# A second set of residual staging tiles for the down projection, kept in a quarter of the up projection's result

## The chip, the cores and the metric

The kernel runs on all 8 NeuronCores of one Trainium2 chip: two dies, cores 0 to 3 and cores 4 to 7. The cores share no data. The time of a run is that of its slowest core, in microseconds (us) on the device.

Runs come in two states. In the slow one, a die (sometimes both) runs at a lower granted TensorE clock (the share of full clock that the profile's clock record shows) and the run is longer. In the first job, the slowest run after the change took 5593.35 us, with die 0 at 0.812 or 0.813 and die 1 at 0.991 or 0.992. The fast runs are those in which no die is disturbed: the two after the change in that job took 4757.07 and 4761.27 us, with 0.990 to 0.994 on all cores.

## The reference, cut to what matters

The program is two layers of a mixed diffusion backbone. Only the end of each layer matters here, the MLP with its residual:

```python
    # channel mixer: squared-ReLU MLP
    h2 = _rms(x) * (1 + sc2) + sh2
    x = x + g2 * (jnp.square(jax.nn.relu(h2 @ w_ff1)) @ w_ff2)
```

`D_MODEL` is 2048, `D_FF` is 8192, and each core has 1280 tokens. The kernel does `D_FF` in four quarters `q`. For each it computes 2048 hidden channels (up projection), then adds their contribution to `x` (down projection).

## The kernel before

The kernel is a graph of operations that a list scheduler in Python puts into a fixed order for each of five engines, using guessed durations. Each list is then the program of its engine, in that order, with the semaphore waits in it. For a transfer the scheduler guesses this:

```python
                st = max(now + o.dur + 1.2, dma_free[0])
                en = st + o.dma / self.bw          # bw = 320e3 bytes per us
                dma_free[0] = en
                o.t1 = en + 0.9
```

For the 160 KB transfers that matter here that is about 2.7 us: 0.08 issue, 1.2 + 0.9 fixed, 0.51 for 163,840 bytes. On core 0 of the profile before, the medians from issue to landing were 6.0 us for these loads and 6.3 us for the spills.

Both projections use a Strassen-like scheme, seven block products in place of eight. A unit makes 2 x 128 output channels for all 1280 tokens: 7 products x 2 token halves x 8 chunks = 112 matmuls of 128x128 by 128x320. A down projection is 8 units.

```python
                prods = (("P", w8(ra, 0), ra, "B11", True), ("Q", w8(ra, 1), ra, "B21", True), ("P", k8(s2), s2, 1, False), ("R", k8(s1), s1, 0, True),
                         ("P", k8(s3), s3, 2, False), ("P", w8(rb, 1), rb, 3, False), ("R", k8(s4), s4, "B22", False))
```

The operand (`act`, 16 rows of 1280 columns) is read as the quarters B11, B21 and B22 and as four sums. The quarter B12, rows 0 to 7, columns 640 to 1280, is read only when the sums are made. After that its space is free. The kernel uses B12 of the up projection's operand `hT` as eight staging tiles for the residual `x`, which lives in DRAM (`xs`). Each unit loads eight pieces of `x`, adds the product on VectorE (DVE), and spills them back:

```python
            XSt = [hT[:, i, 640:1280].bitcast(F32) for i in range(8)]
            # ... (res: x = product * gate + x on DVE)
            def pre_f2(ba, bb):                       # before a unit: its eight loads
                for s_ in range(2):
                    for k, (blk, c) in enumerate(((ba, s_ * SUBS), (ba, 640 + s_ * SUBS), (bb, s_ * SUBS), (bb, 640 + s_ * SUBS))):
                        load(XSt[s_ * 4 + k], xs[blk][:, c:c + SUBS], 128 * SUBS * 4, r=xkeys(blk, c, SUBS), prio=S.p + 50, tag="xld")

            def epi_f2(dst):
                def f(blk, c, b, ps, s_, k):          # when a block of the product is done
                    x = XSt[s_ * 4 + k]
                    res(x, b, ps, *gcol(blk), c)
                    spill(blk, c, SUBS, x, dst)
                return f
```

Loads and spills are all issued by SyncE, in one program order. Weights are issued by GpSimd. Seven of the eight down projections (56 units) use these tiles. The last one of layer 0 works on tiles that stay in SBUF.

Of the kernel before, what the change touches and what calls it, by code (L numbers as in the profile page):

```python
# [8 lines left out]
F32 = mybir.dt.float32  # L9
# [473 lines left out]
T = 1280  # L483
# [46 lines left out]
def build():  # L530
# [36 lines left out]
    xs = nc.dram_tensor("xs", [16, 128, T], F32, kind="Internal").ap()  # L567
# [5 lines left out]
    with es:  # L573
        arena = es.enter_context(nc.sbuf_tensor("arena", [128, int(TOTKB * 512)], F16))
        psum = es.enter_context(nc.psum_tensor("psum", [128, 4096], F32))
        S = Graph(nc, es)

        def A(kb, shape, dt=F16):
            n = 1
            for s in shape:  # L580
                n *= s
            o = int(round(kb * 512))
            ne = n * DSZ[dt] // 2
            assert o + ne <= int(TOTKB * 512), (kb, shape)
            v = arena[:, o:o + ne]
            if dt != F16:
                v = v.bitcast(dt)
            if len(shape) == 1:
                return v
            if len(shape) == 2:  # L590
                return v.rearrange("p (a b) -> p a b", a=shape[0])
            return v.rearrange("p (a b c) -> p a b c", a=shape[0], b=shape[1])
# [62 lines left out]
        hT = A(0, [16, T])  # L655
# [25 lines left out]
        def load(dst, src, nb, q="sp", r=(), w=None, prio=None, tag="ld"):  # L681
            return S.dma(q, dst, src, nb, r=r, w=[dst] if w is None else w, prio=(S.p if prio is None else prio) - 60.0, tag=tag)
# [1111 lines left out]
        SUBS = 320  # L1794

        def xkeys(fc, t0, n):
            return ["xs%d_%d" % (fc, j) for j in range(t0 // SUBS, (t0 + n - 1) // SUBS + 1)]
# [5 lines left out]
        def spill(fc, t0, n, src, dst=None):  # L1803
            d = xs if dst is None else dst
            S.dma("sp", d[fc][:, t0:t0 + n], src, 128 * n * 4, r=[src], w=xkeys(fc, t0, n) if dst is None else [], tag="xst")
# [5 lines left out]
        def tsums(act, Ts, i):  # L1811
            b11, b12 = act[i][:, 0:640], act[i][:, 640:1280]
            b21, b22 = act[i + 8][:, 0:640], act[i + 8][:, 640:1280]
            t1, t2, t3, t4 = (t[:, i, :] for t in Ts)
            for o, x, y in ((t1, b12, b11), (t3, b22, b12), (t2, b22, t1), (t4, b21, t2)):
                tt("dve", o, x, y, ALU.subtract, 640, [x, y], [o], x=2)
# [90 lines left out]
        def layer(l):  # L1907
# [61 lines left out]
            def epi_f1(blk, c, b, ps, s_, k):  # L1969
# [9 lines left out]
                i = blk % 8  # L1979
                if done1.get(i, 0) == 4 and done1.get(i + 8, 0) == 4:  # L1980
                    tsums(M, ATs, i)
            XSt = [hT[:, i, 640:1280].bitcast(F32) for i in range(8)]

            def res(x, b, ps, g0, g1, c):

                cuts = [(0, SUBS, 0)] if c < 960 else [(0, 64, 0), (64, SUBS, 1)]
                for (u, v, s) in cuts:
                    i = b[:, u:v] if b is not None else (lambda u=u, v=v: ps.ap()[:, u:v])
                    g = (g0, g1)[s]
                    stt_(x[:, u:v], i, g, x[:, u:v], ALU.mult, ALU.add, v - u, [b if b is not None else ps, x[:, u:v]], [x[:, u:v]], ps=b is None, boost=BOOST)  # L1990

            def gcol(blk):
                return [modT[l][:, s, 80 + blk:80 + blk + 1] for s in range(2)]

            def pre_f2(ba, bb):
                for s_ in range(2):
                    for k, (blk, c) in enumerate(((ba, s_ * SUBS), (ba, 640 + s_ * SUBS), (bb, s_ * SUBS), (bb, 640 + s_ * SUBS))):
                        load(XSt[s_ * 4 + k], xs[blk][:, c:c + SUBS], 128 * SUBS * 4, r=xkeys(blk, c, SUBS), prio=S.p + 50, tag="xld")

            def epi_f2(dst):  # L2000
                def f(blk, c, b, ps, s_, k):
                    x = XSt[s_ * 4 + k]
                    res(x, b, ps, *gcol(blk), c)
                    spill(blk, c, SUBS, x, dst)
                return f
# [16 lines left out]
            for q in range(4):  # L2022
                done1 = {}
                if not last:
                    if q == 0:
                        mod_push(1, (0, 1, 2))
                    mod_spread(12, 9.0)
                pair1 = lambda i: (i, i + 8, w1[l, q * 16 + i], w1[l, q * 16 + i + 8])
                pair2 = lambda i: (i, i + 8, w2[l, q, i], w2[l, q, i + 8])
                if q == 0:  # L2030
                    head = [0, 8, 1, 9, 2, 10]
                    b1 = [(b, w1[l, b]) for b in head]
                    dense(b1[:5], H, ev_f1, group=5, tag="ff1")
                    dense(b1[5:], H, ev_f1, tag="ff1")
                    for i in range(3):
                        tsums(M, ATs, i)
                    sunits([pair1(i) for i in range(3, 8)], H, HTs, epi_f1, tag="sf1")
                else:
                    sunits([pair1(i) for i in range(8)], H, HTs, epi_f1, tag="sf1")
                if q < 3 or last:  # L2040
                    sunits([pair2(i) for i in range(8)], M, ATs, epi_f2(None if q < 3 else y_o), pre=pre_f2, tag="sf2")
                else:
                    reload_x(range(8), xs, True)
                    sunits([(i, i + 4, w2[l, q, i], w2[l, q, i + 4]) for i in range(4)], M, ATs, epi_x, tag="sf2")
                    reload_x((10, 11, 12, 13, 8, 9, 14, 15), xs, True)
                    e2 = ev_res(l, 80, after_x)
                    dense([(b, w2[l, q, b]) for b in (10, 11, 12)], M, e2, tag="ff2")
                    dense([(b, w2[l, q, b]) for b in (13, 8, 9, 14, 15)], M, e2, group=5, tag="ff2")
# [3 lines left out]
        for l in range(NL):  # L2052
            layer(l)
# [226 lines left out]
```

## Time and profile before

| | before |
|---|---|
| fast runs of the first job | 4810.74, 4820.74, 4815.32 us |
| core 0, an undisturbed core of the profiled run | span 4831.3 us, TensorE busy 4604.6 us |
| its idle time before the product line L1882 | 45.5 us |
| waits of DVE for loads of `xs` | 159.1 us |
| waits of SyncE for spills to `xs` to land | 379.9 us |

The profiled run of before was in the slow state: die 1 was throttled (median clock of its cores 0.930, against 0.983 on die 0). So the readings come from core 0, on die 0. Its page, part 5 (out<-in, shape, count, then busy us and mean ns, then the idle time before the group and what ended most of it), says of the MLP's matmuls and of the group with DVE's residual additions (it holds some other work of the same line too):

```profile
L1882 PE MATMUL psum<-arena 128*128 128x320 f16 x13216 | 1832.5, 302 | 45.5 <-ACT arena L770 38.9
...
L759 DVE SCALAR_TENSOR_TENSOR arena<-arena 128x320 f32<-128x320 f32 (+11 forms) x677 | 359.7, 556 | 297.5 <-DMA arena<-xs 136.7
```

The view of waits of the same core has, for DVE and for SyncE (us in total, times, longest):

```profile
DVE arena L759 <- DMA arena<-xs: 159.1, 133, 6.0
SPq L438 <- DMA xs<-arena: 379.9, 217, 14.0
```

TensorE waited 45.5 us here, 38.9 of them for a ScalarE copy that frees a PSUM bank (PSUM is what the matmuls write, `psum<-arena`). That copy is not the cause. In the first down projection (1601 to 1734 us) DVE's biggest wait is for loads of `xs`, 30.0 us, and the ScalarE copies in turn wait longest for DVE's additions, 64.7 us. The cause shows when the chain of waits is followed back. Part 4 for the same core:

```profile
## 4 chain that ended last, share of the span: by engine, by line
PE 77%; DMA 16%; DVE 2%; issue 2%; SPq 2%; ACT 1%; POOL 1%; DVEq 0%; ACTq 0%; POOLq 0%
```

And a piece of that chain within the first down projection (start us, us, what):

```profile
1614.23 8.34 DMA xs<-arena
1622.56 0.02 issue
...
1622.63 0.32 SPq L222
...
1623.04 6.85 DMA xs<-arena
...
1630.36 8.29 DMA xs<-arena
...
1639.13 6.07 DMA xs<-arena
...
1645.26 6.43 DMA arena<-xs
...
1651.78 0.06 DVE arena L759
```

For 37 us nothing but transfers decides the time. A spill lands, SyncE (`SPq L222`) issues the load that stood waiting for it, then the spill that stood behind that load, and so on. In the end DVE waits for a load.

### The profile page before, as it was taken

To read this page: it belongs to the slowest core of one execution; us is meant where nothing else is said; L and a number is where in the kernel's file an instruction comes from. 1 tells how busy PE (TensorE), PEld (TensorE's weight loads), DVE (VectorE), ACT (ScalarE), POOL (GpSimd) and SP (SyncE) were. 2 spreads that over 40 slices of the span, in tenths; PEclk is the share of its full clock that TensorE was granted. 3 is DMA by queue.
4 is the path that set the end of the run, shared out by engine and by line. 5 is a ranking of instruction groups with operands and counts; after the bars stand their busy time and mean duration, and the time that the engine had idled before them with its cause. 6 is when DMAs were issued, how large, how long until landed. Compare 5 with 4: busy or idle time off the path is not lost.

```text
span 5042.2 us, 91205 instructions; the slowest of 8 cores (4811.6 to 5042.2 us)
## 1 busy us (share of the span) xinstructions
PE 4866.5 (97%) x31452; PEld 2977.5 (59%) x31452; DVE 2633.1 (52%) x5454; ACT 1791.0 (36%) x3781; POOL 506.9 (10%) x916
## 2 busy tenths in 40 slices
PE   3989999999999999999999999999999999999999
PEld 2544455556655666666654545555565566666666
DVE  4266645565454545454563565556553555454545
ACT  2235333332235242333443353333321532424151
POOL 1131210001001010000011301000010000000000
PEclk9989999999889989898899999999998899989899
DMA  9873763447857877878777645334666457474837
GB/s 206 133 137 84 151 109 69 84 85 144 175 121 120 189 144 169 164 148 177 149 174 129 120 107 103 64 71 85 133 114 175 95 117 177 101 192 81 213 65 197
DMA packets 339444, 664.37 MB, mean 132 GB/s; under 512 B 51888, under 2 KB 210352, under 8 KB 338992
## 3 DMA queue, kind: packets, MB, share of 16 engines
q0 software_dynamic: 106848, 368.10, 44.9%
q1 hardware_dynamic: 232144, 290.45, 18.3%
q8 instruction: 259, 4.24, 0.4%
q14 instruction: 193, 1.58, 0.1%
HBM read 894.07 MB, written 132.38 MB: 204 GB/s over the span
## 4 chain that ended last, share of the span: by engine, by line
PE 90%; DMA 5%; DVE 2%; issue 1%; SPq 1%; ACT 1%; POOL 0%; DVEq 0%; ACTq 0%; POOLq 0%
PE psum L1882 37%; PE psum L693 23%; PE psum L1698 17%; PE psum L1663 5%; PE psum L1219 1%; PE psum L827 1%; PE psum L1094 1%; DMA arena<-wm 1%; DMA xs<-arena 1%; PE psum L1076 1%; DMA arena<-lc 1%; DMA arena<-wg 1%; DVE arena L755 1%; SPq L222 1%; PE psum L1096 1%
## 5 line engine op out<-in xcount | busy, mean ns | idle before, releaser
L1882 PE MATMUL psum<-arena 128*128 128x320 f16 x13216 | 1980.2, 318 | 3.7 <-ACT arena L770 3.7
L1882 PEld LDWEIGHTS psum<-arena 128*128 128x128 f16 x13216 | 1357.1, 103 | 621.7 <-issue 15.7
L755 DVE TENSOR_TENSOR arena<-arena 128x1024 f16<-128x1024 f16 (+10 forms) x2162 | 1073.8, 519 | 692.2 <-PE psum L1882 354.3
L693 PE MATMUL psum<-arena 128*128 128x512 f16 (+2 forms) x6272 | 1284.9, 368 | 12.9 <-DVE arena L759 7.3
L744 ACT ACTIVATE arena<-arena 128x320 f16<-128x320 f32 (+12 forms) x1679 | 832.6, 515 | 906.4 <-DVE arena L755 517.0
L755 DVE TENSOR_TENSOR arena<-psum,arena 128x320 f32<-128x320 f32 (+3 forms) x1406 | 684.0, 490 | 825.0 <-PE psum L1882 263.3
L693 PEld LDWEIGHTS psum<-arena 128*128 128x128 f16 x6272 | 635.4, 103 | 615.4 <-issue 297.3
L1698 PE MATMUL psum<-arena 128*128 128x320 f16 x6272 | 973.7, 306 | 15.4 <-ACT arena L744 10.1
L770 ACT COPY arena<-psum 128x320 f32<-128x320 f32 (+5 forms) x987 | 422.9, 435 | 1378.0 <-PE psum L1882 725.0
L1698 PEld LDWEIGHTS psum<-arena 128*128 128x128 f16 x6272 | 603.9, 99 | 333.3 <-issue 96.0
L744 ACT ACTIVATE arena<-psum 128x320 f16<-128x320 f32 (+6 forms) x562 | 279.8, 499 | 750.0 <-PE psum L693 465.0
L759 DVE SCALAR_TENSOR_TENSOR arena<-arena 128x320 f32<-128x320 f32 (+11 forms) x677 | 359.7, 557 | 233.4 <-POOL arena L1265 71.8
L759 DVE SCALAR_TENSOR_TENSOR arena<-arena,psum 128x320 f16<-128x320 f16 (+2 forms) x516 | 259.9, 504 | 320.7 <-ACT arena L744 205.9
L1663 PE MATMUL psum<-arena 128*128 128x320 f16 x1792 | 326.1, 308 | 14.4 <-DVE arena L759 9.3
L222 POOL DMA_DIRECT2D arena<-w x256 | 135.4, 529 | 1760.5 <-PE psum L1882 1152.1
L744 ACT ACTIVATE arena<-psum,arena 128x512 bf16<-128x512 f32 x320 | 205.3, 682 | 112.8 <-PE psum L1076 112.2
L1663 PEld LDWEIGHTS psum<-arena 128*128 128x128 f16 x1792 | 172.4, 100 | 106.7 <-issue 38.6
L759 DVE SCALAR_TENSOR_TENSOR arena<-psum,arena 128x320 f32<-128x320 f32 (+2 forms) x240 | 144.8, 603 | 146.4 <-PE psum L693 132.9
L222 POOL DMA_DIRECT2D arena<-wm x176 | 94.6, 538 | 805.3 <-PE psum L827 304.8
L222 POOL DMA_DIRECT2D arena<-wg x128 | 68.0, 532 | 874.0 <-PE psum L1698 634.7
L755 DVE TENSOR_TENSOR arena<-arena,psum 128x512 f16<-128x512 f32 (+2 forms) x164 | 97.1, 606 | 27.4 <-ACT arena L744 13.2
L770 ACT CAST arena<-psum 128x512 f16<-128x512 f32 (+1 forms) x124 | 62.9, 552 | 64.6 <-PE psum L693 40.3
(102 smaller groups left out, 1229.8 us busy)
## 6 DMA issues: line engine op xcount, KB each, us to landing
arena<-w POOLq DMA_DIRECT2D x256, 512.0 KB, 6.9
arena<-wm POOLq DMA_DIRECT2D x176, 512.0 KB, 7.0
arena<-xs SPq DMA_DIRECT2D x448, 160.0 KB, 6.0
arena<-wg POOLq DMA_DIRECT2D x128, 512.0 KB, 6.3
xs<-arena SPq DMA_DIRECT2D x384, 160.0 KB, 6.2
xs<-arena SPq DMA_DIRECT2D x96, 256.0 KB, 3.1
arena<-xin SPq DMA_DIRECT2D x32, 640.0 KB, 23.7
arena<-xs SPq DMA_DIRECT2D x32, 640.0 KB, 15.7
```

The lines of the kernel that those rows point to most:

```text
L222: return self.op(q, issue, (lambda e, o=out, a=in_, k=kw: e.dma_start(out=lz(o), in_=lz(a), **k)), r, w, prio, dma=nbytes, q=q, tag=tag)
L693: ins = e.matmul(o, lhsT=lhs(kc), rhs=rhs(kc), start=kc == 0, stop=kc == nk - 1)
L744: return e.activation(out=lz(o), in_=lz(i), func=func, scale=scale, **kw)
L755: lambda e: e.tensor_tensor(out=lz(o), in0=lz(a), in1=lz(b), op=op), r=r, w=w, prio=S.p - boost, tag=tag)
L759: lambda e: e.scalar_tensor_tensor(out=lz(o), in0=lz(a), scalar=sc, in1=lz(b), op0=op0, op1=op1),
L770: return S.op("act", tact(n, callable(i)), lambda e: e.copy(out=lz(o), in_=lz(i)), r=r, w=w, prio=S.p - boost, tag=tag)
L827: ins = e.matmul(ps.ap()[32 * j:32 * j + 32, :], lhsT=scT[:, kc, :], rhs=w()[:, 512 * j:512 * j + 512], start=kc == 0, stop=kc == 15)
L1076: ins = e.matmul(sc.ap()[:, hf * 512:hf * 512 + n], lhsT=kT[64 * hf:64 * hf + 64, kb * 128:(kb + 1) * 128], rhs=qT[64 * hf:64 * hf + 64, j ...
L1094: ins = e.matmul(pv.ap()[64 * hf:64 * hf + 64, 0:n], lhsT=V[:, kb, 64 * hf:64 * hf + 64], rhs=PT[:, hf, 0:n], start=ki == 0, stop=ki == nk ...
L1663: ins = e.matmul(pb.ap()[:, 0:SUBS], lhsT=wbv()[:, ri, i, :], rhs=O[:, i, c:c + SUBS], start=i == 0, stop=i == 3)
L1698: ins = e.matmul(ps.ap()[:, 0:SUBS], lhsT=wv_(kc), rhs=rhs(kc), start=new and kc == 0, stop=kc == 7, skip_group_check=True)
L1882: ins = e.matmul(ps.ap()[:, 0:SUBS], lhsT=wv(kc), rhs=rhs(kc), start=first and kc == 0, stop=kc == 7, skip_group_check=True)
```

## The change

The same quarter B12 of the down projection's own operand, the up projection's result `M` (rows 0 to 7 at 50 KB), is free as well once its sums are made. The change uses it as a second set of eight tiles and alternates between the sets unit by unit. A load then has to wait for the spill of two units ago instead of one. Bytes, transfers and arithmetic stay the same.

```diff
-            XSt = [hT[:, i, 640:1280].bitcast(F32) for i in range(8)]
+            XSt = [[t[:, i, 640:1280].bitcast(F32) for i in range(8)] for t in (hT, A(50, [8, T]))]
+            xset = [1]
 ...
             def pre_f2(ba, bb):
+                xset[0] ^= 1
 ...
-                        load(XSt[s_ * 4 + k], xs[blk][:, c:c + SUBS], 128 * SUBS * 4, r=xkeys(blk, c, SUBS), prio=S.p + 50, tag="xld")
+                        load(XSt[xset[0]][s_ * 4 + k], xs[blk][:, c:c + SUBS], 128 * SUBS * 4, r=xkeys(blk, c, SUBS), prio=S.p + 50, tag="xld")
 ...
-                    x = XSt[s_ * 4 + k]
+                    x = XSt[xset[0]][s_ * 4 + k]
```

## The prediction

> **What bounds it now.** Two of three timed runs are fast (4810.7 and 4820.7 us); the page is of a slow-state execution, so I read core 0 of the undisturbed die (4831.3 us, clock 0.981). TensorE is busy 4604.6 us there (95%, part 1 of the page). The view of waits gives its product line L1882 (up and down projection) 45.5 us of idle time, 38.9 of it behind a ScalarE copy out of PSUM. TensorE's timeline puts nearly all of it in the down projections: 6.4, 7.0 and 9.4 us in the three of layer 0 that use the staging tiles, 5.3, 7.1, 4.3 and 5.1 us in the four of layer 1, 44.6 us in all. The up projections between have none. Cores 1 to 3 show 43 to 45 us; the throttled die 0 to 10 us, since a slower TensorE hides it.

> **Why it waits.** The chain of waits is one of transfers there: a spill to xs lands in 6 to 9 us, the load that overwrites its tile is issued, the spill queued behind it follows, and so on, until DVE waits for a load of xs (159 us, 133 waits), which holds back DVE, the ScalarE copies and at last the PSUM banks. SyncE runs in program order: it waits 379.9 us (217 times) for spills to land. [...] In a down projection of layer 1 the queue's groups of three spills recur every 15.1 to 17.8 us, mean about 16.5, while TensorE needs 112 x 137.5 ns = 15.4 us for a unit. So SyncE falls behind by about 1 us per unit and uses up its slack after about three units (first stall at 1639 us, some 40 us in).

> **What the change does.** The same 448 loads, same spills and arithmetic. A load now needs the spill of two units earlier. I expect the static order on SyncE still to put each load shortly after the spill that frees its tile, because the scheduler takes a transfer for about 2.6 us, not 6 to 8. So SyncE still waits for spills and keeps its pace of 16.5 us. What is gained is lead: every load is needed one unit (15.4 us) later. In eight units the queue falls back some 9 us (estimate: 8 x 1.1), less than that lead, and each up projection lets it catch up. So TensorE should run through. The new tiles are next written at the end of the next up projection's units, over 13 us after the last use: no new wait.

> **On the critical path:** 44.6 us of stalls (0.9%), of which 35 to 44 should go; a few may return as lower clock or other order. From the fast mean of 4816 us: about 4776 us. 8 in 10: 4756 to 4808. Faster by over 2%: 0.02; within 2%: 0.96; slower: 0.02.

> **What would show it.** On a fast core: idle before L1882 from 45 us to under 8; DVE's waits for loads of xs from 159 us to under 30; the links "spill, load, spill" gone from the chain, TensorE's share of it from 77% to near 90%. If my step on SyncE's order is right, its waits for spills stay near 380 us (over 250); if they vanish, the order changed. On a throttled die nothing is gained.

> **What would make it wrong.** The clock of the fast die falls as TensorE loses its pauses; the greedy schedule is reordered far from the change; the up projection's first writes, or the subtractions that read the quarter, hold back the second set; SyncE's backlog exceeds one unit.

That the slower TensorE of die 1 hides the stall was read from the same profile: the L1882 matmuls of core 4 were busy 1980.2 us against 1832.5 on core 0, so a unit of 112 took 16.8 us against 15.5, while the stall was 3.7 us against 45.5 and DVE's waits for loads of `xs` were 63.9 us against 159.1.

## The result, and the profile after

The fast runs after were 4761.27 and 4757.07 us, mean 4759.2, against a mean of 4815.6 for the three of before. The ratio is 0.9883, 95% interval 0.9854 to 0.9912. A ratio here is the mean time of one kernel's fast runs over that of the other's fast runs of the same job, so it is not quite the ratio of the medians. The change saved about 56 us. I had said 40.

The other two of the four runs after were slow, which is why the median over all, 4900.57 us, misleads. In one of them die 0 ran at a clock of 0.812 and took 5590 us, while die 1, at 0.99, took 4746 us at most.

The same lines of core 0 after the change, part 5:

```profile
L1882 PE MATMUL psum<-arena 128*128 128x320 f16 x13216 | 1803.0, 299 | 1.1 <-DVE arena L755 1.1
...
L759 DVE SCALAR_TENSOR_TENSOR arena<-arena 128x320 f32<-128x320 f32 (+11 forms) x677 | 359.0, 555 | 164.8 <-POOL arena L1265 66.0
```

And its waits:

```profile
DVE arena L759 <- DMA arena<-xs: 5.2, 15, 2.5
SPq L438 <- DMA xs<-arena: 401.5, 198, 13.1
```

The idle time of TensorE in the MLP fell from 45.5 to 1.1 us, and loads of `xs` are no longer what these additions wait for most. The second thing to see is that the busy time of the same 13,216 matmuls fell too, from 1832.5 to 1803.0 us, although no matmul was taken away. About 8.5 us of these 29.5 are intervals at clock 0.812 that happened to fall into this slow run of before, and are no gain (an estimate: three intervals of 15.1 us in the MLP of layer 1, 0.188 of each; an up projection with one of them took 124 us, one without took 122). I come back to the rest below. The chain (part 4) of the same core, and the chain within its first down projection:

```profile
PE 89%; DMA 5%; DVE 2%; issue 2%; ACT 1%; SPq 1%; POOL 1%; DVEq 0%; ACTq 0%; POOLq 0%
```

```profile
by line: PE psum L1882 100.1%; PE psum L827 0.3%
2 pieces in order of time: start us, us, what
1593.88 122.11 PE psum L1882 x899
```

In place of transfers there is one unbroken piece of TensorE work, 122.1 us long. DVE's waits for loads of `xs` fell from 159.1 to 5.2 us. SyncE's own waits did not go: 379.9 us before, 401.5 us after. They stopped mattering.

The fixed order of the instructions, compared between the two kernels, is the same for TensorE and GpSimd and differs at a few places for DVE (10 of 5454) and ScalarE (5 of 3734). For SyncE it differs at many (883 of 1541). So it was not at once clear whether the lead or the new order was what helped.

### The profile page after: what moved, and what is told of

Same layout as the page of the kernel before. It is cut to its first block, busy times and chain, and to the rows that moved or that the text cites. A ratio compares the mean times of both kernels' runs of the same rounds, so it can differ in the third digit from the quotient of the medians.

```text
span 4759.7 us, 91659 instructions; the slowest of 8 cores (4718.7 to 4759.7 us)
## 1 busy us (share of the span) xinstructions
PE 4560.7 (96%) x31452; PEld 2869.5 (60%) x31452; DVE 2621.0 (55%) x5454; ACT 1785.2 (38%) x3781; POOL 513.0 (11%) x916
## 4 chain that ended last, share of the span: by engine, by line
PE 86%; DMA 7%; DVE 2%; issue 2%; SPq 1%; ACT 1%; POOL 1%; DVEq 0%; ACTq 0%; POOLq 0%
PE psum L1882 35%; PE psum L693 22%; PE psum L1698 17%; PE psum L1663 5%; DMA xs<-arena 2%; DMA arena<-wg 2%; DMA arena<-wm 1%; PE psum L1219 1%; PE psum L1094 1%; DVE arena L755 1%; PE psum L827 1%; PE psum L1076 1%; DMA arena<-lc 1%; SPq L222 1%; DVE arena L759 1%
## 5 line engine op out<-in xcount | busy, mean ns | idle before, releaser
L1882 PE MATMUL psum<-arena 128*128 128x320 f16 x13216 | 1807.3, 299 | 9.6 <-ACT arena L770 9.6
L1882 PEld LDWEIGHTS psum<-arena 128*128 128x128 f16 x13216 | 1290.9, 98 | 521.4 <-issue 20.5
L693 PE MATMUL psum<-arena 128*128 128x512 f16 (+2 forms) x6272 | 1187.5, 349 | 14.3 <-DVE arena L759 6.6
L744 ACT ACTIVATE arena<-arena 128x320 f16<-128x320 f32 (+12 forms) x1679 | 832.1, 515 | 842.5 <-DVE arena L755 470.8
L1698 PE MATMUL psum<-arena 128*128 128x320 f16 x6272 | 946.9, 300 | 17.4 <-ACT arena L744 9.8
L693 PEld LDWEIGHTS psum<-arena 128*128 128x128 f16 x6272 | 609.0, 99 | 548.2 <-issue 52.9
L1698 PEld LDWEIGHTS psum<-arena 128*128 128x128 f16 x6272 | 593.7, 98 | 318.9 <-issue 97.6
L744 ACT ACTIVATE arena<-psum 128x320 f16<-128x320 f32 (+6 forms) x562 | 279.6, 499 | 681.1 <-PE psum L693 409.2
L1663 PE MATMUL psum<-arena 128*128 128x320 f16 x1792 | 317.2, 301 | 15.5 <-DVE arena L759 11.2
L744 ACT ACTIVATE arena<-psum,arena 128x512 bf16<-128x512 f32 x320 | 205.2, 682 | 113.1 <-PE psum L1076 112.4
L1663 PEld LDWEIGHTS psum<-arena 128*128 128x128 f16 x1792 | 168.8, 98 | 104.2 <-issue 40.5
L827 PE MATMUL psum<-arena 128*32 128x512 f16 x704 | 70.1, 394 | 19.3 <-DMA arena<-wm 19.3
```

Source lines behind the costliest of these rows:

```text
L693: ins = e.matmul(o, lhsT=lhs(kc), rhs=rhs(kc), start=kc == 0, stop=kc == nk - 1)
L744: return e.activation(out=lz(o), in_=lz(i), func=func, scale=scale, **kw)
L827: ins = e.matmul(ps.ap()[32 * j:32 * j + 32, :], lhsT=scT[:, kc, :], rhs=w()[:, 512 * j:512 * j + 512], start=kc == 0, stop=kc == 15)
L1663: ins = e.matmul(pb.ap()[:, 0:SUBS], lhsT=wbv()[:, ri, i, :], rhs=O[:, i, c:c + SUBS], start=i == 0, stop=i == 3)
L1698: ins = e.matmul(ps.ap()[:, 0:SUBS], lhsT=wv_(kc), rhs=rhs(kc), start=new and kc == 0, stop=kc == 7, skip_group_check=True)
L1882: ins = e.matmul(ps.ap()[:, 0:SUBS], lhsT=wv(kc), rhs=rhs(kc), start=first and kc == 0, stop=kc == 7, skip_group_check=True)
```

## The experiments

Twelve runs were made, of nine different kernels, in four jobs on four chips. All gave correct results. Two quantities recur:

- *Stall*: idle time of TensorE before its L1882 instructions, the mean over the 8 cores of a fast profile (each gap over 0.05 us added up).
- *The round of a tile*: from the last DVE write of a staging tile to the first DVE use of the next piece of `x` in it. I took it from the traces by pairing each load with the spill it waits for and with DVE's instructions before and after, over the 8 cores of a profile. It is split at the issue and landing of both transfers.

| kernel | sets | data ready to spill issued | spill | landed to load issued | load | landed to use | round | stall |
|---|---|---|---|---|---|---|---|---|
| lead_off (as before) | 1 | 1.93 | 6.07 | 0.66 | 5.77 | 1.44 | 15.87 | 44.1 |
| loads_later | 1 | 0.22 | 5.47 | 4.36 | 5.14 | 1.02 | 16.21 | 59.3 |
| loads_bit_later | 1 | 0.43 | 6.23 | 1.79 | 5.59 | 1.21 | 15.25 | 18.1 |
| bit_again | 1 | 0.40 | 6.25 | 1.83 | 5.46 | 1.26 | 15.19 | 17.4 |
| loads_pool | 1 | 0.09 | 6.70 | 1.26 | 5.77 | 1.52 | 15.35 | 19.9 |
| after_third | 2 | 5.51 | 6.01 | 0.70 | 5.96 | 11.70 | 29.89 | 1.0 |
| both_again | 2 | 0.25 | 5.90 | 2.44 | 6.74 | 14.51 | 29.84 | 0.0 |

Columns are means in us. A unit takes TensorE 112 x about 136 ns = 15.2 us (the 122.1 us piece above divided by 8 is 15.3). With one set, the whole round includes the slack before use and so is simply a unit as it really ran (less DVE's own addition): it grows with the stalls and does not explain them. What can explain them is the sum of the four columns from "data ready" to "load", the time that a tile is not available: 14.4 us in lead_off, 15.2 in loads_later, 14.0, 13.9 and 13.8 in the next three. These are averages, and TensorE stalls where a single tile is late. With two sets it is 18.2 us in after_third, of two units.

### before_again and after_again: the same kernels once more

No edit. These are a control of the measurement.

> The kernel before, unchanged, as an A/A control and for a profile in the fast state, which the first profile was not. Theory (stalls of TensorE in the down projections, plus what follows each of them): ratio 1.000 within 0.3%; about 43 to 46 us idle before the product line L1882 on every core of an undisturbed die; SyncE waits 370 to 390 us for spills to xs; and, at half clock, some granted-clock intervals directly after the longer stalls, costing about 10 us on core 0 as in the first profile. Rival (the gain beyond the stalls, about 15 of 56 us, is a [...]throttle at clock 0.812 that the first profile of before caught): the fast profile of before shows intervals at 0.812 on both dies in the f2 phases, worth 15 us or more, which the changed kernel has not.

Measured: ratio 1.0037 (1.0021 to 1.0053) for the kernel against itself, outside the 0.3% expected. So two sets of runs of one kernel can differ by about 0.4%, more than their interval says, and differences of that size are not read below. Its three fast runs were 4825 to 4840 us. The kernel before in the same job had seven, 4814 to 4820 us. The profile fell in the slow state, so it gives no fast profile of before. lead_off, below, takes that place.

> The changed kernel, unchanged, on this chip, for a common comparison. Ratio to before 0.986 to 0.991; idle before L1882 under 10 us on every core; DVE's waits for loads of xs under 25 us; SyncE's waits for spills still about 400 us.

Measured: ratio 0.9888 (0.9873 to 0.9904). By core, the stall was 0.5 to 12.5 us, one core above the 10 us I gave, and its mean was 4.4 us. DVE's waits for loads of `xs` were 3.8 to 30.5 us, again one core above the 25. SyncE's waits for spills were 344 to 445 us. As expected, but for these two cores. The mean span over all cores of the fast runs fell from 4793.7 to 4736.6 us, by 57 us. So this is a gain of every core and not of the slowest alone.

On the rival: in the fast profiles die 0 has two or three intervals at clock 0.812, about 155 us long in all and before the MLP, before the change (lead_off) as after it (after_again). Die 1 has none in either, and its cores still took 4784.5 us on average in lead_off and 4730.3 us in after_again, 54 us less. So such intervals are not what the change removed.

### lead_off: two sets, but no lead

```diff
-                        load(..., r=xkeys(blk, c, SUBS), ...)
+                        load(..., r=xkeys(blk, c, SUBS) + ["st%d" % (s_ * 4 + k)], ...)
 ...
-                    spill(blk, c, SUBS, x, dst)
+                    spill(blk, c, SUBS, x, dst, ["st%d" % (s_ * 4 + k)])
```

(The spill writes the key, the load reads it, so a load waits for the spill of the same slot one unit earlier although its tile is free.)

> The second set stays and is used in turn, but each load also waits for the spill of the same slot of the unit just before, as with one set (the order on all five engines is then that of the kernel before). Theory (the lead of one unit is the whole gain): same as before, ratio 0.998 to 1.002, idle before L1882 40 to 50 us, SyncE's waits for spills about 380 us. Rival (where the tiles lie[...] is a part of the gain): ratio below 0.996, idle below 35 us.

Measured: ratio 1.0005 (0.9991 to 1.0018), stall 44.1 us, SyncE's waits for spills 372 to 499 us. The order on all five engines is exactly that of before. So where the tiles lie gives nothing. This run takes away the lead and the new order of DVE, ScalarE and SyncE together, so alone it does not tell them apart. Two runs below do in part: last_layer_only keeps DVE's and ScalarE's order of before and still loses the stall in the layer that has two sets, and both_again has another order on SyncE with the same time. Because order and time are those of before, this profile, in the fast state on all cores, serves as the fast profile of before.

### loads_later: one set, loads 4 us later in SyncE's order

After scheduling, each residual load is moved in the global order to where the scheduler's clock reads 4 us more (or half way to its first user, where that is less). The order of the other four engines stays as it was.

```diff
-        self.order = order
-        self.seqs = seqs
+        self.order, self.seqs = loads_later(ops, order)
 ...
+            d = min([4.0] + [0.5 * (ops[j].t0 - o.t0) for j in o.succ])
+        key[i] = (o.t0 + d, o.order)
```

> One set of tiles as before; only SyncE's static order changes: each residual load stands about 4 us later in the scheduler's time, behind the spills that would otherwise queue behind it (order of the other four engines identical). Theory (a load that waits at the head of SyncE's in-order queue for the spill before it holds back the later spills, so SyncE runs at 16.5 us per unit against TensorE's 15.4): SyncE's waits for spills fall from 380 to under 150 us, idle before L1882 falls from 45 to under 10 us, ratio 0.986 to 0.993, without any second set. Rival (one set cannot turn round in a unit: spill 6.6 us plus load 6.2 us plus the wait for the right moment is more than the 15.4 us unit leaves): idle before L1882 stays over 30 us and the ratio is 0.996 to 1.003.

Measured: ratio 1.0029 (1.0015 to 1.0043), stall 59.3 us. Stall and ratio are those that the rival had named (over 30 us, 0.996 to 1.003), and the theory's were missed. SyncE's waits for spills fell to 92 to 155 us, as the theory said, but the stall rose all the same. Core 7, waits of TensorE:

```profile
PE psum L1882 <- ACT arena L770: 51.6, 40, 4.6
```

The round in the table shows another reason than the rival's. Spills were issued at once (0.22 us instead of 1.93), but each load now stood in SyncE's list behind spills whose data DVE had not made yet, and went out 4.36 us after its tile was free (0.66 before). Queueing moved from the spill to the load and grew from 2.6 to 4.6 us in sum. The dose was too large to test the theory, so the run does not decide between theory and rival.

### loads_bit_later and bit_again: the same with 1.5 us

```diff
-            d = min([4.0] + [0.5 * (ops[j].t0 - o.t0) for j in o.succ])
+            d = min([1.5] + [0.5 * (ops[j].t0 - o.t0) for j in o.succ])
```

> As loads_later, but the loads stand 1.5 us later instead of 4. There, spills were issued 0.2 us after their data (2.0 us before), but loads 4.3 us after their spill had landed (0.7 before), so the sum of queueing grew from 2.7 to 4.5 us. If a better single order exists between, the sum is under 2.5 us here, idle before L1882 20 to 40 us, ratio 0.994 to 1.000. If any order of one in-order queue only shifts the wait from the spill to the load, the sum stays 2.5 us or more and the ratio is 0.999 to 1.004.

Measured: ratio 0.9898 (0.9869 to 0.9926) from two fast runs, stall 18.1 us, queueing 0.43 + 1.79 = 2.2 us. The queueing is as expected, and ratio and stall are better than expected.

> loads_bit_later again (one set, loads 1.5 us later), since its first ratio rests on two fast runs: ratio 0.988 to 0.993, idle before L1882 14 to 25 us. It should be slower than the changed kernel by the 10 to 20 us of stalls it keeps; if it is as fast, those stalls are hidden behind something.

Measured: ratio 0.9944 (0.9914 to 0.9973) from four, just above the 0.993 expected, stall 17.4 us, queueing 2.2 us. The mean span of the cores is the same in both, 4757.3 us. It is the kernel before that was faster on the chip of bit_again's job (mean of cores 4789.0 us against 4800.0). Core 7 of bit_again:

```profile
PE psum L1882 <- ACT arena L770: 15.4, 19, 2.2
PE psum L1882 <- DVE arena L755: 0.6, 1, 0.6
```

So with one set of tiles and nothing changed but SyncE's order, more than half of the stall goes. It takes only 0.4 us less queueing per round (2.6 to 2.2): transfers and queueing already filled 14.4 us of a unit of 15.3, so a little decides whether a load is late. The kernel stays slower than the changed one, 4757 against 4730 us, means of the cores in that job. These 27 us are more than the 10 to 20 expected and more than the stalls of 17 us that it keeps. The surplus was not followed up.

### loads_pool: one set, loads issued by another engine

```diff
-                        load(..., prio=S.p + 50, tag="xld")
+                        load(..., prio=S.p + 50, tag="xl2", q="pool")
```

> One set of tiles; the residual loads are issued by GpSimd's queue, the spills stay on SyncE's, so no spill can stand behind a load. In a fast trace with one set the round of a tile, from the last DVE write to the next DVE read, averages 2.0 us until the spill is issued, 6.1 us spill, 0.7 us until the load is issued, 5.8 us load, 1.4 us until use: 16.0 us, and TensorE's unit is 15.4 us. Theory (the 2.7 us of queueing in SyncE's order is what turns 12 us of transfers into more than a unit): queueing falls under 1.5 us, idle before L1882 falls from 43 us to under 15 us, ratio 0.988 to 0.994. Rival (12 us of transfers and DVE's in-order epilogue already fill the unit; only lead helps, whatever queue): idle stays over 30 us, ratio over 0.997. A third outcome, loads stuck behind weight loads on GpSimd, would show as later landings of weights and waits of DVE or TensorE for w.

Measured: ratio 0.9910 (0.9862 to 0.9958), stall 19.9 us (13.3 to 33.5 by core). Queueing fell to 0.09 + 1.26 = 1.35 us, but the spill took 6.70 us in place of 6.07. The load took 5.77 us, as when SyncE issued it in lead_off. The ratio and the queueing are as the theory said, the stall is above its 15 us. Core 7:

```profile
PE psum L1882 <- ACT arena L770: 22.0, 25, 2.7
```

So both causes that loads_later had left open take part. With less queueing, in SyncE's one order or by a second queue, more than half of the stall goes. The rest stayed with both, with about 12 us of a unit in the two transfers alone. Of what was tried, only lead takes that away. (GpSimd's order changed here with the loads, and DVE's at 9 places. TensorE's waits for weights of line L827 were 19.4 us on core 0 against 11.7 in lead_off, a small part of the third outcome.)

### last_layer_only: the second set in one of the two layers

```diff
-            xset = [1]
+            xset = [int(last)]
 ...
-                xset[0] ^= 1
+                xset[0] ^= last
```

> The second set in the last layer alone (32 of 56 units); the first layer keeps one set. Theory (stalls local to each down projection, plus half-clock intervals after the longer ones): in the first layer 20 to 25 us of idle time of TensorE stay in the three down projections, with the granted clock there at 0.96 to 0.99; in the last layer the idle time goes below 4 us and the clock in the down projections is that of the up projections; the ratio is about half-way, 0.9935 to 0.9965. Rival (the gain is a matter of the whole program: static order[...]): the ratio is at one of the ends, or the idle time goes in both layers or in none.

Measured: ratio 0.9946. The interval is wide (0.9855 to 1.0037), with three fast runs of which one was at 4828 us, so the ratio alone would not decide. The profile does. The windows view of core 0, a core of the undisturbed die, has the three down projections of layer 0 and, in the lines after the gap, two of layer 1 with the up projection between them (from:to, length, then busy us and count of TensorE, weight loads, DVE, ScalarE, GpSimd, then the granted clock, DMA share, GB/s):

```profile
1601.00:1734.00 133.00, 125.80 (x904) 88.35 (x902) 77.02 (x161) 21.61 (x52) 8.44 (x16) 0.97 0.88 205
...
1860.00:1991.00 131.00, 125.60 (x898) 88.34 (x896) 75.62 (x158) 21.63 (x52) 8.44 (x16) 0.97 0.87 205
...
2122.00:2251.00 129.00, 124.44 (x904) 87.92 (x902) 76.71 (x160) 21.63 (x52) 8.44 (x16) 0.99 0.90 212
...
3930.00:4052.00 122.00, 122.00 (x901) 87.80 (x899) 77.21 (x163) 22.44 (x53) 8.44 (x16) 1.00 0.89 211
4052.00:4174.00 122.00, 122.00 (x901) 87.89 (x899) 57.19 (x111) 72.32 (x173) 8.44 (x16) 1.00 0.55 102
4174.00:4296.00 122.00, 122.00 (x900) 87.80 (x899) 77.60 (x163) 21.84 (x52) 8.45 (x16) 1.00 0.91 211
```

In one execution on one core, a down projection with one set takes 129 to 133 us and has a granted clock of 0.97 to 0.99. One with two sets takes 122 us, as long as an up projection, at 1.00. The gain is local to each down projection, and clock and stall go together. On all eight cores the stall is 17 to 30 us in layer 0. In layer 1 it is zero on six cores and 4.0 and 5.0 us on two, a little above the 4 us expected. In this kernel the orders of TensorE, ScalarE, DVE and GpSimd are those of before, so the reordering of DVE and ScalarE is not needed for the gain. SyncE's order is different, as it has to be once loads need not wait for the last unit's spills.

### after_loads_later and both_again: two sets and the later loads

The edit of loads_later, on the changed kernel.

> Both: two sets, and loads 4 us later in SyncE's order. Theory (with a lead of one unit neither order matters): same as the changed kernel, ratio to before 0.986 to 0.991, idle before L1882 under 8 us; SyncE's waits for spills under 150 us against 350 to 445, which shows that those waits cost nothing once there is lead.

Measured: ratio 0.9836 (0.9806 to 0.9866) from two fast runs, 4741 and 4748 us, and no stall on any core. The ratio was below the expected range. SyncE's waits for spills were 131 to 211 us on the eight cores, not all under the 150 expected.

> The changed kernel once more, for a comparison on one chip with the two below. Ratio to before 0.986 to 0.991, idle before L1882 0 to 13 us by core, as in its first two profiles.

> after_loads_later again (two sets, and the loads 4 us later in SyncE's order), to see whether it beats the changed kernel: its two fast runs were 4741 and 4748 us, those of the changed kernel 4755 to 4771. If the last stalls (3 to 13 us on the slowest cores) are what remained: ratio to before 0.983 to 0.987, 5 to 15 us below the changed kernel, no idle time before L1882. If the difference was chance: ratio 0.986 to 0.991, within 4 us of the changed kernel.

Measured in one job on one chip: the changed kernel 4746.6 to 4753.3 us (four fast runs, ratio 0.9877, 0.9845 to 0.9910), the two together 4735.7 to 4765.3 us (three runs, ratio 0.9884, 0.9841 to 0.9927). The means of the slowest cores are 4750.7 and 4753.6 us, those of all cores 4730.4 and 4729.4 us. So the first ratio was chance, as the second expectation had said. With lead, SyncE's order is worth nothing measurable: the few us of stall left by core go, and SyncE waits 65 to 169 us for spills instead of 323 to 395, without effect on the time. I found no version that beats the changed kernel.

### start_in_m: which unit uses which set

After these runs I looked at where the stalls left in the changed kernel lie. The two longest of its three fast profiles, 8.1 and 9.9 us, are not in a down projection but in the third unit of the up projection behind one. Core 7 of the changed kernel's profile, waits of ScalarE:

```profile
ACT arena L744 <- DMA xs<-arena: 14.4, 4, 10.9
```

And the chain there, up to TensorE's next matmul:

```profile
1728.30 22.73 DMA xs<-arena
1751.08 0.04 issue
1751.12 0.04 ACT arena L744
...
1751.86 0.41 ACT arena L770
...
1752.40 4.42 PE psum L1882 x16
```

ScalarE's L744 writes the up projection's result into `M`, and the quarter it is to write is still being spilled: that one spill took 22.7 us. So there is a new wait, which I had ruled out. Eight units alternate, so the last unit of a down projection uses the set that the first units of the next up projection overwrite. The edit swaps the sets:

```diff
-            xset = [1]
+            xset = [0]
```

> The changed kernel with the two sets swapped: the first unit of a down projection uses the new set (in M), the last one the old (in hT), which the next up projection does not write. Against my prediction, the fast profiles of the changed kernel show a new wait: ScalarE, which writes the up projection's result, waits for late spills out of the new set (0 to 14.4 us by core), and the two longest stalls left (8.1 and 9.9 us) are in an up projection behind it. Theory (those spills are the last unit's): ScalarE's waits for spills to xs go to under 1 us on every core and no stall of over 3 us is left in the second or third unit of an up projection; the mean of the cores changes by less than 5 us (ratio to before 0.984 to 0.992). Rival (the backlog of SyncE reaches back two units): ScalarE still waits for spills. Possible cost: the first unit's loads now wait for the sums that read the quarter, so DVE may wait for xs in first units.

Measured: nearly all runs of this job were slow, for both kernels (before had no fast one), so there is no ratio and the time stays open. The profile has one undisturbed die, die 1, at a clock of 0.99. On its four cores ScalarE never waits for spills to `xs`, no stall is left in an up projection, and DVE's waits for loads are 2.9 to 12.0 us. The one stall over 0.5 us, 3.9 us, is in the last unit of a down projection. So the late spills were those of the last unit, as the theory said.

In the three fast profiles of the changed kernel the new wait stands behind five stalls of 2.9 to 9.9 us on five of 24 cores, 29.1 us in all or 1.2 us per core. That is too little to see in the time. In both_again it does not occur, because SyncE has no backlog there.

### Where the 56 us came from

One core of each, both on undisturbed dies in fast runs, with the down projections cut out by the windows view. Core 7 of lead_off (as before), an up projection and the down projections on both sides of it:

```profile
3897.00:4035.00 138.00, 125.61 (x896) 87.71 (x894) 77.37 (x162) 21.30 (x52) 8.45 (x16) 0.98 0.87 202
4035.00:4157.00 122.00, 122.00 (x900) 87.80 (x898) 57.09 (x111) 72.07 (x173) 8.44 (x16) 1.00 0.44 84
4157.00:4295.00 138.00, 125.98 (x898) 87.97 (x896) 77.58 (x162) 21.35 (x52) 8.46 (x16) 0.98 0.86 200
```

Core 7 of after_third, the same three stretches:

```profile
3874.00:3996.00 122.00, 122.00 (x900) 87.87 (x898) 77.61 (x163) 21.82 (x52) 8.44 (x16) 1.00 0.91 218
3996.00:4117.00 121.00, 121.00 (x893) 87.18 (x891) 56.54 (x110) 71.76 (x172) 8.44 (x16) 1.00 0.49 95
4117.00:4239.00 122.00, 122.00 (x900) 87.87 (x898) 77.59 (x163) 22.16 (x53) 8.45 (x16) 1.00 0.91 213
```

The up projections are equal. Each of the two down projections became 16 us shorter. About 12 us of it is idle time (138 minus 125.6 busy) and nearly 4 us is busy time (125.6 to 122.0) for the same matmuls. The busy time goes with the granted clock, 0.98 against 1.00. Over all seven down projections of this core the length falls by 68 us: 50 us of stall and 18 us of busy time.

Most of this busy time is a cost of the stalls themselves (12 of 18 us per core, worked out below). TensorE's timeline of lead_off's core 7 at the end of the first of these down projections (start, us, what, count, idle before it and what ended that):

```profile
4012.31 5.59 PE L1882 MATMUL psum<-arena 128*128 128x320 f16 x40 [0.35 <-DVE arena L755]
4021.57 18.63 PE L1882 MATMUL psum<-arena 128*128 128x320 f16 x117 [3.67 <-ACT arena L770]
```

The windows view around that pause of 3.67 us:

```profile
4008.00:4018.00 10.00, 9.55 (x70) 6.48 (x67) 4.22 (x9) 0.56 (x2) 0.53 (x1) 1.00 0.88 197
4018.00:4025.00 7.00, 3.43 (x14) 1.91 (x15) 4.04 (x9) 0.96 (x3) 0.53 (x1) 0.64 0.84 255
4025.00:4035.00 10.00, 10.00 (x68) 6.89 (x67) 5.58 (x12) 1.60 (x4) 0.53 (x1) 0.91 0.90 231
```

In the window with the pause the clock is 0.64, and 3.43 us of work does 14 matmuls, against 70 in 9.55 us just before. In the next window it is still 0.91. The trace's clock record has an interval at 0.5 there from 4020.0 to 4026.9 us, 5.3 us of it after the pause.

Nearly all intervals at 0.5 in these traces last 3.41 us or a multiple of it. Shorter pauses than that had half clock with them too. I counted the pauses before L1882 of over 0.5 us in five fast profiles with one set of tiles (lead_off, loads_later, loads_bit_later, bit_again and the two-layer mix of last_layer_only, 8 cores each; loads_pool, whose 80 pauses look alike, was left out), and how many have an interval at 0.5 during them or beginning within 1.5 us after:

| pause, us | pauses | with half clock | mean half-clock time after the pause, us |
|---|---|---|---|
| 0.5 to 2 | 641 | 7 | under 0.11 |
| 2 to 2.5 | 70 | 35 | 1.87 |
| 2.5 to 3 | 45 | 31 | 2.44 |
| 3 to 3.5 | 25 | 21 | 2.99 |
| over 3.5 | 27 | 27 | 4.4 |

Summed over TensorE's busy time from the first MLP on, half clock cost 21.9 us per core in lead_off, 9.7 us in after and after_again, and 9.3 us in after_third. What is left lies mostly outside the down projections. So 12 us went with the stalls. Together with 40 to 43 us less stall (from 44.1 to between 1.0 and 4.4) that makes 52 to 56 us per core, against a measured 57 us (mean of cores, after_again's job) and 59 us (after_third's). The busy time of the L1882 matmuls fell by more than these 12 us: from a mean of 1821.9 us in lead_off to 1804.2 in after_again, 18 us. So some 6 us of busy time went with the stalls without a half-clock record, and stay unexplained.

## Why the prediction was right, and where it was short

- **What bounds the kernel, and why TensorE waits**: right. The seven down projections held nearly all of the stall (44.1 us per core in a fast profile). lead_off shows that the second set without lead removes none of it, and last_layer_only that it goes in just those down projections that have lead. loads_bit_later and loads_pool show that queueing on SyncE was more than half of its cause.
- **"SyncE still waits for spills and keeps its pace"**: right. Its waits were 380 us before and 323 to 466 us in the three fast profiles after. The backlog shows in the round: with two sets a spill goes out 5.5 us after its data on average, and a tenth of them about 11 us or later. By unit of a down projection (profile of after, all cores) it is 0.9, 2.8, 4.8, 6.6, 8.6, 10.0, 10.7 and 9.2 us, with spills about 17 us apart from unit to unit until the fifth, against TensorE's 15.3. In lead_off, where DVE has to wait for SyncE, it stays near 2 us, and in both_again at 0.2. I had estimated 9 us by the end of eight units and a lead of 15.4 us. Loads landed 11.7 us before use on average. But single spills went out up to 27 us late, and "SyncE's backlog exceeds one unit", which I had named as what would make the prediction wrong, came true for these. Single loads of the later units then landed just before use.
- **"TensorE should run through"**: right for most cores. The stall was under 8 us on 18 of the 24 cores of three fast profiles and 8.0 to 12.5 us on six. DVE's waits for loads of `xs` were under 31 us on all, under 30 on all but one. TensorE's share of the chain of core 0 went from 77% to 89%. So "under 8 us" held on three cores of four.
- **"No new wait"** from the up projection's writes to the second set: wrong, at a small price. I counted 13 us from the last use to the first write, and did not set against it the backlog of about 9 us that I had just worked out, plus the spill itself. A late last spill (up to 22.7 us) then holds ScalarE and TensorE. It cost 1.2 us per core on average, and start_in_m removes it.
- **The size**: short by 17 us (4776 predicted, 4759 the mean of the fast runs, inside my range but near its low end). The term that was mis-sized is "a few may return as lower clock or other order". I took TensorE's own work as fixed and feared that a busier TensorE would be granted less. It was the other way round: the mean granted clock of dies 0 and 1 (medians of their cores) was 0.984 and 0.989 in lead_off and 0.987 and 0.992 in after_again. Pauses of over 2 us often had half clock after them (114 of 167), so 12 us of work time, and some 6 us more that no clock record explains, went with the stalls. The evidence was in the profile before. The windows view of a down projection shows a clock of 0.97 to 0.99 between up projections at 1.00 (in core 0's own trace of before in the second and third, though not in the first), and I did not price it.
- **"On a throttled die nothing is gained"**: left open. I read it from the 0 to 10 us of stall there, and slow runs are not compared here.

That half clock goes with the pauses is shown by the clock records and by one core that has both kinds of down projection in one execution. No run inserted pauses of chosen lengths, so the 0.5 to 0.6 of a window is an observation from 808 pauses and from the windows of the clock's grid, not an experiment.

## What to carry to other kernels

A staging tile's round (spill, load and the queueing of both) has to be shorter than the work between two uses, with room to spare. With 14.4 us of transfers and queueing on average in a unit of 15.3 TensorE stalled 44 us, with 13.8 to 14.0 it still stalled, less than half as much, and a second set brought the same transfers, in the same slow queue, down to 1 to 4 us. Before buying a second set, look at the static order on the issuing queue: here a load whose tile was not yet free held back the spills behind it (SyncE waited 372 to 499 us for spills in lead_off), and moving it 1.5 us took away more than half of the stall (44.1 to 18.1 us), while moving it 4 us made things worse (59.3 us). Give the last use before a phase change to the buffer that the next phase does not write. When you price pauses of TensorE, add what comes after them: here, pauses of over 2 us mostly had half clock after them (114 of 167), and the whole gain was about 1.4 us for each microsecond of stall saved.
